# Attention's split and values one and two steps later, and v turned by VectorE through a DRAM scratch instead of TensorE

## The chip, the cores and the metric

The kernel runs on one core of a Trainium2 chip. The time is the device time of one execution in microseconds (us); a version is told by the median over its runs. Beside it stands one profiled execution, with a trace of every instruction and DMA.

## The reference

One layer of a streaming encoder on 320 frames (256 of a prompt and 64 of a running stream), D = 2048, all in float32:

```
xn = RMSNorm(x)
h  = xn @ w_in                     # columns [u 2048 | v 2048 | q 2048 | k 256 | v_attn 256]
u, v = gelu(h[u]), gelu(h[v])
a  = u * (ws_masked @ LayerNorm(v) + bs)       # mixes tokens inside chunks of 128
o  = windowed attention of q on k, v_attn      # 32 heads of 64, 4 groups, rope, sinks
x  = x + (sigmoid(xn @ w_gate_a) * (a @ w_a) + sigmoid(xn @ w_gate_b) * (o @ w_b)) @ w_out
x  = x + (silu(RMSNorm(x) @ w_fg) * (RMSNorm(x) @ w_fu)) @ w_fd
y  = RMSNorm(x)                    # outputs also: new keys, new values, LayerNorm(v) of the 64 frames
```

What matters here is v: LayerNorm runs over its 2048 features, and the mixing runs over tokens, so v is needed with tokens on the partitions, while a product leaves it with features on the partitions.

## The kernel before

**Products.** Activations lie with features on the partitions: `xh` and `xl` (high and low part, [128, 16, 320]). `gemm` (from L136 on) makes 512 output features at a time: four PSUM banks of [128, 320], and for each pair of 128-row blocks of the weight it loads [128, 2, 512] floats (`raw`, 512 KB, `fetch`, issued on SyncE's queue, SP), splits it (`prepare`, `split`: ScalarE copies the high part `hi`, L107; VectorE subtracts to make the low part `lo`, L110) and runs 24 matmuls, three for each product of two parts (L151 to L153). The split runs two blocks ahead, the fetch six; there are four `raw` and three `hi` and `lo` buffers.

**Order.** After every 12 matmuls `pump` is called: one slot. `later(n, fn)` writes fn into a calendar, n slots on; at that slot fn's instructions are put into the program. A product of 16 rows of weight has 16 slots. Engines run their queues in order; the program order comes from this calendar, and a scheduler that models the engines may let an instruction whose inputs it holds ready pass one on the same engine that waits. The products come in the order k and v_attn ("kv"), q0, q1, v0, q2, v1, q3, v2, v3, then the four of w_gate for B (gb), of w_branch_b (bb), u, w_gate for A, w_branch_a, w_out and the feed-forward part.

**Attention.** `q_done(g)` begins when the product of q group g is done; `QK0[g]` slots later come the scores of the first of five query chunks, and a chunk every 5 slots. `attend` gives the steps of a chunk with their slots: scores 0 (eight matmuls, maxima, exp into `pr`), weigh 2, pack 3 (VectorE transposes 32x32 blocks of `pr` into `u`, L498), spread 4 (four DMAs on SP write `u` to a DRAM scratch `pd`, L507), gather 6 (one or two DMAs on SP read it back as `pf` with keys on the partitions, L516), part 9 (splits `pf` into `ph` and `pl`, and a half block into `p`), values 11 (two or three matmuls into the bank `o`, L539; ScalarE copies one half, VectorE adds, L541 and L547).

**v.** `v_done(g)` begins when the product of v group g is done. VectorE multiplies by the norm's factor (L577), ScalarE applies gelu (L578). Slots 3 to 6 turn one of the four tiles each: three TensorE transposes into the bank `vt` (L583), a VectorE copy of 256 columns (L585) and a ScalarE copy of 128 (L586) into `tok`, which holds tokens on the partitions. At slot 8 come the statistics for LayerNorm (`stats`, L592).

**After v3.** `at` is 16: `open_late` opens the next pool, `split_o` splits the attention output in eight steps for bb, `v_aggr` joins the statistics, `v_norm` normalises v.

Of the kernel before, what the change touches and what calls it, by code (L numbers as in the profile page):

```python
# [10 lines left out]
F32 = mybir.dt.float32  # L11
F32R = mybir.dt.float32r
AF = mybir.ActivationFunctionType
# [5 lines left out]
P = 128  # L19
D = 2048  # L20
DC = D // P
T = 320
TS = 64
F = 5632
FC = F // P
W = 512
# [8 lines left out]
    [(0, 4), (512, 4), (1024, 4), (1536, 2), (1792, 2)],  # L35
]
QV = [("q", 0), ("q", 1), ("v", 0), ("q", 2), ("v", 1), ("q", 3), ("v", 2), ("v", 3)]
QK0 = [14, 24, 18, 13]

NK = [64, 128, 192, 192, 192]  # L40
KC = [0, 0, 0, 64, 256]
# [3 lines left out]
def f32(ap):  # L45
    return ap.bitcast(F32)
# [23 lines left out]
def tile_hybrid_step(ctx: ExitStack, tc: tile.TileContext, a: dict, outs: list):  # L70
    nc = tc.nc
    y_p, y_s, ko_p, vo_p, ko_s, vo_s, gv_s = outs
    w_in, w_gate = a["w_in"][0], a["w_gate"][0]
# [7 lines left out]
    dram = ctx.enter_context(tc.tile_pool(name="dram", bufs=1, space=DRAM))  # L81

    def bank(name):
        return psum.tile([P, 512], F32, tag="bank", name=name)
# [5 lines left out]
    def later(slots, fn):  # L90
        calendar.setdefault(now[0] + max(1, slots), []).append(fn)
# [13 lines left out]
    def split(hi, lo, src, eng=None):  # L105
        if eng is None:
            nc.scalar.activation(hi, src, AF.Copy)  # L107
        else:
            eng.tensor_copy(hi, src)
        nc.vector.tensor_tensor(lo, src, f32(hi), op=ALU.subtract)  # L110


    plan = []
    for w, c0, k0, nk, nt in products(a):
        plan += [(w, c0, k0 + kb, nt) for kb in range(0, nk, 2)]
    raws, parts = {}, {}
    at_block = [0]

    def fetch(j):
        if j < len(plan):  # L120
# [4 lines left out]
                w[k * P : (k + 2) * P, c0 : c0 + nt * P].rearrange("(c p) m -> p c m", p=P),  # L125
            )

    def prepare(j, eng=None):
        if j < len(plan):
            n = plan[j][3] * P  # L130
            hi = wpool.tile([P, 2, W], F32R, tag="hi", name=f"hi_{j}", bufs=PARTS)
            lo = wpool.tile([P, 2, W], F32R, tag="lo", name=f"lo_{j}", bufs=PARTS)
            split(hi[:, :, :n], lo[:, :, :n], raws.pop(j)[:, :, :n], eng)
            parts[j] = hi, lo

    def gemm(w, c0, xh, xl, name, k0=0, nk=DC, nt=4):  # L136
        ps = [bank(f"mm_{name}_{t}") for t in range(nt)]
        for kb in range(0, nk, 2):
            j = at_block[0]
            at_block[0] += 1  # L140
            assert plan[j][1:] == (c0, k0 + kb, nt)
            if j + PARTS - 1 not in parts:
                prepare(j + PARTS - 1)
            fetch(j + PARTS - 1 + RAWS)
            hi, lo = parts.pop(j)
            for t in range(nt):
                cols = slice(t * P, (t + 1) * P)
                for c in range(2):
                    k = kb + c
                    o = ps[t][:, :T]  # L150
                    nc.tensor.matmul(o, hi[:, c, cols], xh[:, k, :], start=(k == 0), stop=False)  # L151
                    nc.tensor.matmul(o, hi[:, c, cols], xl[:, k, :], start=False, stop=False)  # L152
                    nc.tensor.matmul(o, lo[:, c, cols], xh[:, k, :], start=False, stop=(k == nk - 1))  # L153
                if nt == 1 or t % 2 == 1:
                    pump()
        return [p[:, :T] for p in ps]


    ident = main.tile([P, P], F32, name="ident")
# [6 lines left out]
    tok = main.tile([P, 3, D], F32, name="tok")  # L166
# [6 lines left out]
    xs = [(i, P if i < 2 else TS) for i in range(3)]  # L173
# [96 lines left out]

    x_in(0)
    prepare(0, nc.vector)
    x_in(1)
    fetch(RAWS)
    x_keep(0)
    x_in(2)
    prepare(1)
    fetch(RAWS + 1)
    for k in range(3, DC):
# [49 lines left out]
    def rope_turn(t0):  # L329
        t1 = tmp.tile([P, 2, T], F32, tag="st", name="rope_t1")  # L330
        cb = cos_t.unsqueeze(1).broadcast_to([P, 2, T])
        sb = sin_t.unsqueeze(1).broadcast_to([P, 2, T])
        q2 = qr[:, t0 : t0 + 2, :]
        nc.vector.tensor_tensor(q2, q2, cb, op=ALU.mult)
        nc.vector.tensor_tensor(t1, swp[:, t0 : t0 + 2, :], sb, op=ALU.mult)
        nc.vector.tensor_tensor(q2, q2, t1, op=ALU.add)
# [118 lines left out]
    def attend(g, n, qs, st):  # L455
# [38 lines left out]
        nb = nk // 32  # L494
# [54 lines left out]
                    pov[0:64, e], olv[:, e], op=ALU.add  # L549
                )  # L550

        return ((0, scores), (2, weigh), (3, pack), (4, spread), (6, gather), (9, part), (11, values))

    def q_done(g, ps):
        for t in range(4):
            nc.scalar.activation(qr[:, t, :], ps[t], AF.Copy)
        qs = ap.tile([P, 20, 2, 64], F32R, tag="qs", name=f"qs_{g}")
        hi, lo = q_parts(g, qs)
        later(1, lambda: rope_swap(4))
        later(5, lambda: rope_turn(0))  # L560
        later(7, lambda: rope_turn(2))
        at = QK0[g]
        later(at - 5, lambda: hi(0))
        later(at - 4, lambda: lo(0))
        later(at - 3, lambda: hi(1))
        later(at - 2, lambda: lo(1))
        for n in range(5):
            for dt, step in attend(g, n, qs, {}):
                later(at + 5 * n + dt, step)
# [4 lines left out]
    def v_done(g, ps):  # L574
        for t in range(4):
            v = tmp.tile([P, T], F32, tag="e1", name=f"v_{g}_{t}", bufs=4)
            nc.vector.tensor_tensor(v, ps[t], rx, op=ALU.mult)  # L577
            nc.scalar.activation(v, v, AF.Gelu_apprx_tanh)  # L578

            def turn(t=t, v=v):  # L580
                pt = bank(f"vt_{g}_{t}")
                for i, n in xs:
                    nc.tensor.transpose(pt[:n, i * P : (i + 1) * P], v[:, i * P : i * P + n], ident)  # L583
                c = slice((4 * g + t) * P, (4 * g + t + 1) * P)
                nc.vector.tensor_copy(tok[:, 0:2, c], pt[:, 0:256].rearrange("p (i c) -> p i c", i=2))  # L585
                nc.scalar.activation(tok[0:64, 2, c], pt[0:64, 256:384], AF.Copy)  # L586

            later(3 + t, turn)

        def stats():  # L590
            for i, n in xs:
                nc.vector.bn_stats(bst[:n, i, g, :], tok[:n, i, g * W : (g + 1) * W])  # L592

        later(8, stats)

    for c, g in QV:
        if c == "q":
            q_done(g, gemm(w_in, 2 * D + g * W, xh, xl, f"q{g}"))
        else:
            v_done(g, gemm(w_in, D + g * W, xh, xl, f"v{g}"))  # L600
# [13 lines left out]
    def split_o(m):  # L614
        for k in range(m, m + 2):
            split(late["yh"][:, k, :], late["yl"][:, k, :], f1[:, k, :])
# [36 lines left out]
            nc.vector.memset(late["wst"][64:128, :, 0:64], 0.0)  # L653

    at = 16
    later(at - 3, open_late)
    for k in range(0, DC, 2):
        later(at - 3 + k // 2 + 1, lambda k=k: split_o(k))
    later(at + 3, v_aggr)
    for g in range(4):  # L660
        later(at + max(1, 9 * g - 2), lambda g=g: v_load(g))
# [20 lines left out]
    for g in range(4):  # L682
        ps = gemm(w_bb, g * W, yh, yl, f"bb{g}")
        for t in range(4):
            m = 4 * g + t
# [48 lines left out]
    for g in range(4):  # L734
        ps = gemm(w_ba, g * W, yh, yl, f"ba{g}")
        for t in range(4):
            m = 4 * g + t
# [21 lines left out]
    for g in range(4):  # L759
        ps = gemm(w_out, g * W, xh, xl, f"wo{g}")  # L760
        for t in range(4):
            m = 4 * g + t
# [46 lines left out]
    for nf in FPARTS:  # L809
        for g in range(nf // 4):  # L810
            c0 = f0 * P + g * W
# [13 lines left out]
        for c0, nt in DOWN[last]:  # L825
            ps = gemm(w_fd, c0, xh, xl, f"fd{f0}_{c0}", k0=f0, nk=nf, nt=nt)
            for t in range(nt):
                m = c0 // P + t
# [26 lines left out]
    for h in range(2):  # L855
        c = slice(h * D // 2, (h + 1) * D // 2)
# [61 lines left out]
```

## Time and profile before

| | us |
|---|---|
| median of 3 runs | 1968.05 (1966.51 to 1968.14) |
| the profiled execution, its own time | 1968.4 |
| its span, first to last instruction | 1966.6 |
| mean granted TensorE clock | 0.995 |
| kv product begins | 8.5 |
| q0 to v3 (eight products) | 46.5 to 319.4 |
| gb (four products) | 319.4 to 441.1 |
| bb (four products) | 441.1 to 553.7 |

A row of the page or of a view names line, engine and operation, then the tile written and the tiles read, then shapes and the count. PE is TensorE's matmuls, PEld its weight loads, DVE VectorE, ACT ScalarE, POOL GpSimd, SP SyncE's queue; a q behind the engine stands for its sequencer. In a row of waits stands who waited for whom: us in total, how often, and the longest. In a timeline stand start and length in us; in square brackets the idle time ahead of it and what ended it. Matmuls are pipelined: the length of one is not its cost; the distance of two starts is.

### The profile page before, as it was taken

To read this page: it belongs to the slowest core of one execution; us is meant where nothing else is said; L and a number is where in the kernel's file an instruction comes from. 1 tells how busy PE (TensorE), PEld (TensorE's weight loads), DVE (VectorE), ACT (ScalarE), POOL (GpSimd) and SP (SyncE) were. 2 spreads that over 40 slices of the span, in tenths; PEclk is the share of its full clock that TensorE was granted. 3 is DMA by queue.
4 is the path that set the end of the run, shared out by engine and by line. 5 is a ranking of instruction groups with operands and counts; after the bars stand their busy time and mean duration, and the time that the engine had idled before them with its cause. 6 is when DMAs were issued, how large, how long until landed. Compare 5 with 4: busy or idle time off the path is not lost.

```text
span 1966.6 us, 31779 instructions
## 1 busy us (share of the span) xinstructions
PE 1937.0 (98%) x13179; PEld 1924.8 (98%) x13179; DVE 1042.1 (53%) x1527; ACT 813.6 (41%) x1220; POOL 4.7 (0%) x12
## 2 busy tenths in 40 slices
PE   9999999999999999999999999999999999999996
PEld 8999989999999999999999999999999999999996
DVE  5778887953444543455465444443444444444454
ACT  5566766633333443333343333333333333333343
POOL 0000000000000000000000000000000000000000
PEclk9999999999999999999999999999999999999998
DMA  8555666754444444445445555445555544555433
GB/s 268 155 160 171 181 169 170 218 159 153 147 142 137 138 150 150 150 150 203 150 150 151 150 150 150 150 150 150 150 149 147 154 149 150 146 151 149 152 130 102
DMA packets 169457, 307.41 MB, mean 156 GB/s; under 512 B 11313, under 2 KB 28673, under 8 KB 169121
## 3 DMA queue, kind: packets, MB, share of 16 engines
q1 hardware_dynamic: 164256, 293.64, 49.2%
q10 hardware_dynamic: 5056, 11.74, 1.9%
q8 instruction: 103, 1.69, 0.4%
q14 instruction: 42, 0.34, 0.1%
HBM read 292.15 MB, written 12.45 MB: 155 GB/s over the span
## 4 chain that ended last, share of the span: by engine, by line
PE 82%; DVE 0%; ACT 0%; issue 0%; DVEq 0%
PE mm_fd L151 5%; PE mm_fu L151 5%; PE mm_fg L151 5%; PE mm_fd L153 5%; PE mm_fu L153 5%; PE mm_fg L153 5%; PE mm_fg L152 5%; PE mm_fu L152 5%; PE mm_fd L152 5%; PE mm_u L151 2%; PE mm_bb L151 2%; PE mm_bb L153 2%; PE mm_ba L152 2%; PE mm_ga L152 2%; PE mm_wo L152 2%; PE mm_wo L153 2%
## 5 line engine op out<-in xcount | busy, mean ns | idle before, releaser
L110 DVE TENSOR_TENSOR lo<-raw,hi 128x1024 fp32r<-128x1024 f32 (+1 forms) x534 | 646.2, 1211 | 661.9 <-ACT hi L107 660.4
L107 ACT ACTIVATE hi<-raw 128x1024 fp32r<-128x1024 f32 (+1 forms) x533 | 559.4, 1050 | 1023.4 <-PE mm_fu L152 188.8
L151 PE MATMUL mm_fd<-xh,hi 128*128 128x320 f32 x704 | 218.2, 310 | 0.0
L151 PE MATMUL mm_fg<-yh,hi 128*128 128x320 f32 x704 | 217.8, 309 | 0.0
L153 PE MATMUL mm_fg<-yh,lo 128*128 128x320 f32 x704 | 217.5, 309 | 0.0
L151 PE MATMUL mm_fu<-yh,hi 128*128 128x320 f32 x704 | 217.5, 309 | 0.0
L152 PE MATMUL mm_fu<-yl,hi 128*128 128x320 f32 x704 | 217.5, 309 | 0.0
L153 PE MATMUL mm_fu<-yh,lo 128*128 128x320 f32 x704 | 217.5, 309 | 0.0
L152 PE MATMUL mm_fg<-yl,hi 128*128 128x320 f32 x704 | 217.5, 309 | 0.0
L153 PE MATMUL mm_fd<-xh,lo 128*128 128x320 f32 x704 | 217.1, 308 | 0.0
L152 PE MATMUL mm_fd<-xl,hi 128*128 128x320 f32 x704 | 217.1, 308 | 0.0
L151 PEld LDWEIGHTS mm_fg<-yh,hi 128*128 128x128 f32 x704 | 132.2, 188 | 0.1
L152 PEld LDWEIGHTS mm_fg<-yl,hi 128*128 128x128 f32 x704 | 132.2, 188 | 0.1
L153 PEld LDWEIGHTS mm_fg<-yh,lo 128*128 128x128 f32 x704 | 132.2, 188 | 0.0
L151 PEld LDWEIGHTS mm_fu<-yh,hi 128*128 128x128 f32 x704 | 132.1, 188 | 0.0
L152 PEld LDWEIGHTS mm_fu<-yl,hi 128*128 128x128 f32 x704 | 132.1, 188 | 0.0
L153 PEld LDWEIGHTS mm_fu<-yh,lo 128*128 128x128 f32 x704 | 132.1, 188 | 0.0
L152 PEld LDWEIGHTS mm_fd<-xl,hi 128*128 128x128 f32 x704 | 132.1, 188 | 0.0
L151 PEld LDWEIGHTS mm_fd<-xh,hi 128*128 128x128 f32 x704 | 132.1, 188 | 0.0
L153 PEld LDWEIGHTS mm_fd<-xh,lo 128*128 128x128 f32 x704 | 132.1, 188 | 0.0
L151 PE MATMUL mm_q<-xh,hi 128*128 128x320 f32 x256 | 81.3, 318 | 0.0
L151 PE MATMUL mm_u<-xh,hi 128*128 128x320 f32 x256 | 80.3, 314 | 0.0
(256 smaller groups left out, 3935.2 us busy)
## 6 DMA issues: line engine op xcount, KB each, us to landing
raw<-in_w_in_dram SPq DMA_DIRECT2D x104, 512.0 KB, 3.8
raw<-in_w_ffn_gate_dram SPq DMA_DIRECT2D x88, 512.0 KB, 3.6
raw<-in_w_ffn_up_dram SPq DMA_DIRECT2D x88, 512.0 KB, 3.6
raw<-in_w_ffn_down_dram SPq DMA_DIRECT2D x82, 512.0 KB, 3.6
raw<-in_w_gate_dram SPq DMA_DIRECT2D x64, 512.0 KB, 3.7
raw<-in_w_branch_b_dram SPq DMA_DIRECT2D x32, 512.0 KB, 3.7
raw<-in_w_branch_a_dram SPq DMA_DIRECT2D x32, 512.0 KB, 3.7
raw<-in_w_out_dram SPq DMA_DIRECT2D x32, 512.0 KB, 3.9
```

The lines of the kernel that those rows point to most:

```text
L107: nc.scalar.activation(hi, src, AF.Copy)
L110: nc.vector.tensor_tensor(lo, src, f32(hi), op=ALU.subtract)
L151: nc.tensor.matmul(o, hi[:, c, cols], xh[:, k, :], start=(k == 0), stop=False)
L152: nc.tensor.matmul(o, hi[:, c, cols], xl[:, k, :], start=False, stop=False)
L153: nc.tensor.matmul(o, lo[:, c, cols], xh[:, k, :], start=False, stop=(k == nk - 1))
```

## The change

Four things.

1. In `attend`, part moves from slot 9 to 10 and values from 11 to 13. Group q3 begins its chunks one slot earlier (`QK0[3]` 12 instead of 13).
2. The turn of v leaves TensorE. `turn` is now three VectorE transposes of 32x32 blocks per tile, two of [128, 128] and one of [128, 64], which write `tok` at every fourth element (16 bytes apart). Then `spread` (slot 7) issues twelve DMAs on SP that write the blocks to a DRAM scratch `vd`, in runs of 128 floats, and `gather` (slot 9) two DMAs on SP that read it back into `tok`, and GpSimd clears rows 64 to 127 of the last token block. `stats` moves from slot 8 to 13.
3. The columns of the v weights are interleaved as they are split: tile t of a v product holds every fourth column, 4m + t. `hi` and `lo` of the 32 v blocks are written in order, but `raw` is read in steps of four floats (16 bytes) by ScalarE and VectorE.
4. `open_late` and the eight `split_o` come one slot later.

```diff
-QK0 = [14, 24, 18, 13]
+QK0 = [14, 24, 18, 12]
...
+    def is_v(j):
+        w, c0, _, _ = plan[j]
+        return w.shape == w_in.shape and D <= c0 < 2 * D
...
-            split(hi[:, :, :n], lo[:, :, :n], raws.pop(j)[:, :, :n], eng)
+            h, l, r = hi[:, :, :n], lo[:, :, :n], raws.pop(j)[:, :, :n]
+            if is_v(j):
+                h, l = (x.rearrange("p c (t m) -> p c t m", t=4) for x in (h, l))
+                r = r.rearrange("p c (m t) -> p c t m", t=4)
+            split(h, l, r, eng)
...
-        return ((0, scores), (2, weigh), (3, pack), (4, spread), (6, gather), (9, part), (11, values))
+        return ((0, scores), (2, weigh), (3, pack), (4, spread), (6, gather), (10, part), (13, values))
...
             def turn(t=t, v=v):
-                pt = bank(f"vt_{g}_{t}")
-                for i, n in xs:
-                    nc.tensor.transpose(pt[:n, i * P : (i + 1) * P], v[:, i * P : i * P + n], ident)
-                c = slice((4 * g + t) * P, (4 * g + t + 1) * P)
-                nc.vector.tensor_copy(tok[:, 0:2, c], pt[:, 0:256].rearrange("p (i c) -> p i c", i=2))
-                nc.scalar.activation(tok[0:64, 2, c], pt[0:64, 256:384], AF.Copy)
+                vb = v.rearrange("p (b r) -> p b r", r=32)
+                for i in range(2):
+                    nc.vector.transpose(blocks[:, i, :, :, t], vb[:, 4 * i : 4 * i + 4, :])
+                nc.vector.transpose(blocks[:, 2, 0:2, :, t], vb[:, 8:10, :])
...
+        c = slice(g * W, (g + 1) * W)
+        blocks = tok[:, :, c].rearrange("p i (b c t) -> p i b c t", b=4, t=4)
+        vd = dram.tile([T, W], F32, tag="vd", name=f"vd_{g}", bufs=2)
+
+        def spread():
+            for a_ in range(4):
+                r, x = slice(32 * a_, 32 * a_ + 32), slice(128 * a_, 128 * a_ + 128)
+                for i, nb in ((0, 4), (1, 4), (2, 2)):
+                    nc.sync.dma_start(
+                        vd[P * i : P * i + 32 * nb, x].rearrange("(b r) x -> r b x", r=32),
+                        tok[r, i, c].rearrange("p (b x) -> p b x", b=4)[:, 0:nb, :],
+                    )
+
+        def gather():
+            nc.gpsimd.memset(tok[TS:P, 2, c], 0.0)
+            nc.sync.dma_start(tok[:, 0:2, c], vd[0:256, :].rearrange("(i p) x -> p i x", p=P))
+            nc.sync.dma_start(tok[0:TS, 2, c], vd[256:T, :])
...
-        later(8, stats)
+        later(7, spread)
+        later(9, gather)
+        later(13, stats)
...
-    later(at - 3, open_late)
+    later(at - 2, open_late)
     for k in range(0, DC, 2):
-        later(at - 3 + k // 2 + 1, lambda k=k: split_o(k))
+        later(at - 2 + k // 2 + 1, lambda k=k: split_o(k))
```

## The prediction

> **What bounds the kernel now.** I read the page first, then busy time by stretches, the waits of TensorE, its timeline around the longest waits, and last the rows of the operations that are exchanged.
>
> ```profile
> span 1966.6 us, 31779 instructions
> ## 1 busy us (share of the span) xinstructions
> PE 1937.0 (98%) x13179; PEld 1924.8 (98%) x13179; DVE 1042.1 (53%) x1527; ACT 813.6 (41%) x1220; POOL 4.7 (0%) x12
> ```
>
> TensorE bounds the whole, so an edit counts only by what it adds to or takes from TensorE's row. The next rows, busy time in three stretches, show where that row holds more than dense products: the eight q and v products, the four gb products, and the four bb products beside which nothing else runs on TensorE.
>
> ```profile
> 46.50:319.40 272.90, 265.07 (x1785) 258.57 (x1784) 214.86 (x411) 176.01 (x409) 0.00 (x0) 0.99 0.59 169
> 319.40:441.10 121.70, 119.17 (x808) 117.23 (x807) 89.54 (x146) 62.34 (x96) 0.00 (x0) 1.00 0.62 185
> 441.10:553.70 112.60, 112.60 (x769) 112.60 (x769) 45.92 (x49) 35.04 (x35) 0.00 (x0) 1.00 0.46 150
> ```
>
> The columns are: stretch, its length, busy time of PE, PEld, DVE, ACT and POOL, granted clock, DMA share, GB/s. Four dense products take 112.6 us, so one takes 28.15 and one of its 192 matmuls 0.147. Eight take 225.2, but the first stretch lasts 272.9: 47.7 us go to attention, turns, waits and a clock of 0.99. The second has 9.1 us of the same. All that the change can win is in these 57 us. TensorE is idle in 272.90 - 265.07 = 7.8 and 121.70 - 119.17 = 2.5 us of them. The waits of TensorE between 106 and 352 us name this idle time:
>
> ```profile
> PE o L539 <- ACT ph L107: 4.9, 3, 2.4
> PE o L539 <- DVE p L110: 3.2, 6, 1.2
> PE vt L583 <- ACT pr L478: 1.3, 1, 1.3
> PE o L539 <- DVE pl L110: 0.8, 3, 0.3
> ```
>
> The sum is 10.2 of 10.3 us. The values matmuls (o) wait 8.9 us for the split probabilities ph, pl and p; a turn of v waits once for a PSUM bank that the exp of attention (pr) still reads. TensorE's timeline shows what may follow a long wait:
>
> ```profile
> 146.89 0.49 PE L539 MATMUL o<-ph,vv 128*128 128x512 f32 x1 [1.47 <-ACT ph L107]
> ...
> 149.83 0.47 PE L151 MATMUL mm_q<-xh,hi 128*128 128x320 f32 x1
> 150.10 0.47 PE L152 MATMUL mm_q<-xl,hi 128*128 128x320 f32 x1
> ...
> 287.93 0.50 PE L539 MATMUL o<-ph,vv 128*128 128x512 f32 x1 [2.41 <-ACT ph L107]
> ```
>
> After the first wait, dense matmuls start 0.27 us apart instead of 0.147. The next rows, the same columns by stage (v0, q2, v1, q3, v2, v3, and the first product gb0), show a clock of 0.96 in q2 and 0.95 in v3, the stages of these two waits.
>
> ```profile
> 106.60:139.10 32.50, 31.90 (x222) 31.37 (x221) 23.33 (x48) 18.30 (x54) 0.00 (x0) 1.00 0.59 169
> 139.10:178.60 39.50, 37.19 (x240) 35.50 (x239) 33.15 (x64) 28.85 (x67) 0.00 (x0) 0.96 0.56 164
> 178.60:212.50 33.90, 32.70 (x224) 31.82 (x224) 29.19 (x53) 22.25 (x52) 0.00 (x0) 1.00 0.67 191
> 212.50:247.40 34.90, 34.62 (x237) 33.43 (x236) 27.73 (x59) 24.20 (x62) 0.00 (x0) 1.00 0.59 166
> 247.40:283.50 36.10, 35.08 (x238) 34.03 (x237) 31.82 (x57) 22.79 (x54) 0.00 (x0) 1.00 0.66 178
> 283.50:319.60 36.10, 33.69 (x225) 33.06 (x224) 25.43 (x54) 23.98 (x60) 0.00 (x0) 0.95 0.55 160
> 319.60:352.00 32.40, 29.87 (x197) 27.95 (x196) 24.91 (x46) 22.09 (x44) 0.00 (x0) 1.00 0.62 177
> ```
>
> A clock of 0.96 over 39.5 us loses 1.6 us, and of 0.95 over 36.1 about 1.8; I take 1.5 each. The VectorE column is the second thing to see: 195.6 of 245.4 us, and 33.15 of 39.5 in q2. TensorE is the bound, but VectorE is close behind it here.
>
> **Turns off TensorE.** One turn now stands in TensorE's timeline like this:
>
> ```profile
> 154.25 0.31 PE L153 MATMUL mm_q<-xh,lo 128*128 128x320 f32 x1
> 154.40 0.49 PE L583 MATMUL vt<-ident,v 128*128 128x128 f32 x3
> 154.65 0.40 PE L151 MATMUL mm_q<-xh,hi 128*128 128x320 f32 x1
> 154.88 0.31 PE L152 MATMUL mm_q<-xl,hi 128*128 128x320 f32 x1
> ```
>
> From 154.40 to 154.88 there are 0.48 us, of which one dense matmul would take 0.147. A turn costs 0.33, sixteen cost 5.3 us, and these go whatever else happens, for nothing on TensorE replaces them. The bank wait of 1.3 us goes too: no turn asks for a PSUM bank any more. **The turns' new price** lies on VectorE and SyncE. The rows are the copies that go (from the rows of vt), transposes of two sizes, and the weight split of a block (from the rows of raw):
>
> ```profile
> L585 DVE COPY tok<-vt x16: 383/418/426, 151.9 to 339.0; 128x256 f32<-128x256 f32 x16
> L586 ACT ACTIVATE tok<-vt x16: 250/270/273, 154.1 to 339.5; 64x128 f32<-64x128 f32 x16
> L498 DVE STREAM_TRANSPOSE u<-pr 128x768 f32<-128x768 f32 x12 | 11.7, 973 | 0.6 <-ACT pr L492 0.3
> L498 DVE STREAM_TRANSPOSE u<-pr 128x256 f32<-128x256 f32 x4 | 1.8, 442 | 1.7 <-ACT pr L492 1.7
> L107 ACT ACTIVATE hi<-raw x55: 1042/1059/1098, 108.6 to 347.9; 128x1024 fp32r<-128x1024 f32 x55
> L110 DVE TENSOR_TENSOR lo<-raw,hi x55: 1160/1219/1227, 109.7 to 349.4; 128x1024 fp32r<-128x1024 f32 x55
> ```
>
> A transpose costs (973 - 442) / 512 = 1.04 ns an element over a base of 176. A turn has two of 128 elements (309 ns) and one of 64 (243): 0.86 us, 13.8 for sixteen, against 16 x 0.418 = 6.7 for the copies. VectorE gains 7.1 us of work; ScalarE loses 16 x 0.27 = 4.3. Their writes step 16 bytes, which no row shows; if each element cost twice, 320 x 1.04 ns x 16 = 5.3 us more.
>
> **Interleaved columns.** The 32 blocks of v are split from raw read in steps of 16 bytes. No row of this trace reads SBUF at such a step. The bounds for lo are 1.22 us, the contiguous row, and 1.22 + 1024 x 1.04 ns = 2.28, a second element time for each element. I take the first, since no row shows an element of f32 costing two; I keep the second as a rival, for it decides the sign. [...]
>
> **Queues.** SyncE (SP) gets twelve spreads and two gathers for each v, on the queue that fetches the weights and carries attention's own scratch.
>
> ```profile
> ACT ph L107 <- DMA pf<-pd: 6.9, 7, 2.3
> SPq L123 <- DVE lo L110: 84.6, 37, 5.8
> L507 SPq DMA_DIRECT2D pd<-u x80: 312/441/1307, 108.9 to 338.8; - x80
> pd<-u SPq DMA_DIRECT2D x48, 96.0 KB, 3.5
> raw<-in_w_in_dram SPq DMA_DIRECT2D x42, 512.0 KB, 4.5
> pf<-pd SPq DMA_DIRECT2D x16, 256.0 KB, 4.2
> ```
>
> Twelve issues at 0.44 take 5.3 us, then the gather waits some 3.5 us for the last landing, and behind it in SP stand the weight fetches and the next pd and pf. A fetch has four blocks of 24 x 0.147 = 3.5 us before its split, 14.1, less 4.5 for landing and 0.4 for issue: 9.2 us of room (the 84.6 us row shows SP waiting for buffers, not the reverse). One fetch stands between spread and gather, the next behind the gather; each is late by some 4 us, 6 to 7 where a pd and a pf stand among them. I cost this at nothing. It is tight for attention of q3 beside the turn of v2: spreads and pf at slot 135, gather at 137, pd at 138. At 2 us a slot, pd goes out about 5 us late, and pf lands near 21 us after slot 135 where its part is due at 18. ScalarE then waits 3 us at ph, with later weight splits queued behind it; values has three slots, 6 us, against 3 + 2.6 for the four splits. It just fits: 1 us for it. GpSimd's clearing of the unused rows waits for the spreads; its queue is empty there and no soon work reads them, so nothing. The later statistics, the later late pool and the output splits (one slot) end well before bb reads them: nothing.
>
> **Part one slot, values two slots later.** ScalarE waits 6.9 us in seven places for pf, at most 2.3. A slot is 12 dense matmuls, 1.76, with the extras about 2. One more slot before part covers all but the end of these waits; one more between part and values covers the 1.2 us of p and 0.3 of pl. Of 8.9 us I take 7. With those waits I let both low-clock stretches go, 3.0 us; only the two longest waits were followed by one (the 1.2 and 1.3 us ones were not). If the first comes from something else, 1.5 stays.
>
> **The sum.** -5.3 (turns) - 1.3 (bank) - 7 (values) - 3 (clock) = -16.6. VectorE then has 195.6 + 7.1 = 202.7 us in 228.8, 89%, and q2 needs 33.15 + 1.8 of it in a stage of about 34.4: I put back 3 us there and 1 for the late pf. That makes -12.6. The profiled execution took 1968.4 us, 1.8 more than its span and 0.35 over the median of 1968.05; 1968.4 - 12.6 = 1955.8, so 1956. Own range: 1950 (nothing put back, all 8.9 us gone) to 1962.
>
> **Rivals.** (1) *The strided read costs a second element time, and VectorE becomes the bound.* 32 x 1.06 = 34 us more: 202.7 + 34 = 237 us in a stretch that TensorE could do in 229. Stage by stage the need is about 37 in q2 and v1 and 40 in v2, against 39.5, 33.9 and 36.1 now. At 95% busy, 237 / 0.95 = 249 instead of 245.4; with idle left as chains need it, up to 256: 1972 to 1979, most likely 1974. It decides from where VectorE passes 95% of 229 = 217 us, that is 15 us over 32 blocks, or a lo of 1.7 us. Lo-buffers two blocks ahead soften it, and stages with room (q3, v0) take some: part of its chance lies at no change or a small gain. For it: nothing measured here speaks against it. [...] (2) *The waits only move.* Values stay late because ScalarE and VectorE, in order and fuller, are late by two slots as well, or pf is late behind the spreads. Then only the turns and the bank pay: -6.6, 1962, between 1959 and 1966. For it: releasers ph and p are these two engines. Against: no wait was over 2.4 us, and up to 4 are given. (3) *The change does not take effect in the queue*: values move in program order, but TensorE's queue may keep them where they were. That gives the same 1962 and I count it with (2).
>
> **Numbers.** Forecast 0.46, rival 1 0.37, rival 2 with 3 0.17. Some 0.2%, 3.9 us, is what a measurement of this kernel tells from no change. Faster by more: 0.45 + 0.08 + 0.12 = 0.65. Within: 0.01 + 0.12 + 0.04 = 0.17. Slower: 0.17 + 0.01 = 0.18. The range reaches from 1950 over rival 2 to 1975, which takes in the larger half of rival 1; the likeliest case alone has 1950 to 1962.
>
> **What would show it.** In the changed profile: no vt rows with v; the q and v stretch near 259 us, its waits of o under 2 us and the clock 1.00; transposes of 0.31 and 0.24 us; hi and lo of v blocks at 1.06 and 1.22. A lo of v over 1.7 us, with VectorE above 95% in v1 and v2 and dense matmuls waiting for lo, proves rival 1; waits of o that stay near 9 us prove rival 2; dense matmuls or hi that wait for raw would prove the cost of the queue wrong.

## The result, and the profile after

The changed kernel takes 1984.52 us in the median of four runs (1983.04 to 1988.78), against 1968.10 before (1966.51 to 1968.59, four runs): 16.4 us slower, a ratio of 1.0088 with a 95% interval of 1.0071 to 1.0106. The forecast was 1956, with a range from 1950 to 1975.

The page after, with the columns of the page before:

```profile
span 1981.3 us, 31766 instructions
...
PE 1938.4 (98%) x13131; PEld 1923.5 (97%) x13131; DVE 1070.5 (54%) x1559; ACT 842.7 (43%) x1204; POOL 6.8 (0%) x16
```

VectorE has 28 us more to do and ScalarE 29 more. For ScalarE the change only took work away, 4.3 us of copies, so that number alone says that something it does became dearer. The rows of raw, between 106 and 370 us of the changed kernel, name it:

```profile
L110 DVE TENSOR_TENSOR lo<-raw,hi x57: 1181/1991/2065, 104.4 to 369.1; 128x1024 fp32r<-128x1024 f32 x57
L107 ACT ACTIVATE hi<-raw x56: 1042/2030/2104, 109.5 to 367.4; 128x1024 fp32r<-128x1024 f32 x56
```

The line numbers of the split are unchanged, so the rows can be held against those of before. The shortest are still 1.04 and 1.18 us: the blocks of q and gb. More than half of the blocks in this region belong to v, so the median is one of theirs: 2.03 us for hi (1.06 before) and 1.99 for lo (1.22). A step of 16 bytes costs ScalarE 0.95 ns more for each of 1024 elements and VectorE 0.75.

Where TensorE's time went shows in busy time by stage: first the q and v products and gb as a whole, then q2, v1, v2 and v3:

```profile
46.50:335.10 288.60, 268.54 (x1758) 259.04 (x1757) 239.78 (x429) 204.46 (x396) 1.57 (x3) 0.97 0.61 171
335.10:456.00 120.90, 116.97 (x788) 115.24 (x787) 93.06 (x160) 63.05 (x94) 0.52 (x1) 1.00 0.67 202
139.20:179.50 40.30, 36.00 (x226) 33.87 (x226) 33.58 (x70) 31.71 (x73) 0.52 (x1) 0.97 0.73 203
179.50:215.50 36.00, 33.61 (x224) 32.29 (x224) 33.21 (x49) 26.18 (x41) 0.00 (x0) 0.99 0.61 170
251.70:293.40 41.70, 34.08 (x211) 32.09 (x209) 34.40 (x50) 31.91 (x48) 0.00 (x0) 0.91 0.58 159
293.40:335.10 41.70, 39.16 (x247) 37.74 (x247) 34.78 (x71) 30.39 (x66) 0.53 (x1) 0.93 0.59 171
```

The first stretch grew from 272.9 to 288.6 us; gb did not grow. Two things are to be seen. TensorE is idle for 20.1 us of the first row instead of 7.8. And the clock column lost more: 0.03 x 40.3 + 0.01 x 36.0 + 0.09 x 41.7 + 0.07 x 41.7 = 8.2 us in these four stages, against 3.4 before. The waits of TensorE between 46 and 460 us name the idle time:

```profile
PE o L548 <- ACT ph L107: 6.2, 3, 2.5
PE o L548 <- DVE pl L110: 4.8, 6, 1.4
PE s L473 <- DVE qs L460: 3.2, 1, 3.2
PE mm_gb L160 <- DVE v L586: 2.5, 1, 2.5
PE mm_v L162 <- DVE lo L110: 2.1, 4, 0.9
PE o L548 <- DVE p L110: 1.8, 6, 0.5
PE s L473 <- DVE v L586: 1.3, 1, 1.3
PE mm_q L160 <- ACT pr L487: 1.2, 2, 0.6
PE mm_q L162 <- DVE lo L110: 0.7, 1, 0.7
```

The sum is 23.8 us, 13.6 more than the 10.2 of before. The waits of values (o) did not shrink with two more slots but grew from 8.9 to 12.8. New rows stand beside them: scores wait for the split q (qs) and for VectorE's read of v's bank (v), q and gb products for pr and v, which are no operands of theirs but read PSUM banks, and dense matmuls for lo. All releasers are ScalarE and VectorE. So 13.6 us of waits and 4.8 of clock were lost and 5.3 of turns won: 13.1 of the 14.7 us by which the span grew.

VectorE was not full, though: 33.2 of 36.0 us in v1, 34.4 of 41.7 in v2. Its longest idle time in that region tells why. The first row is of before (106 to 352 us), the second of after (106 to 370):

```profile
DVE lo L110 <- ACT hi L107: 9.2, 12, 1.9
```

```profile
DVE lo L110 <- ACT hi L107: 20.6, 18, 3.0
```

Each lo needs its hi, and hi itself now takes 2.03 us. VectorE stands waiting at the head of its queue: before the lo at 258.99 us it was idle for 2.62 us, and the transpose of a pr that had been ready since 256.7 us began only behind that lo, at 260.90. So what stands behind lo in the queue (pl, p, qs, nm, f) is late though the engine had time for it.

### The profile page after: what moved, and what is told of

It reads as the page before. It is cut to its first block, busy times and chain, and to the rows that moved or that the text cites. A ratio compares the mean times of both kernels' runs of the same rounds, so it can differ in the third digit from the quotient of the medians.

```text
span 1981.3 us, 31766 instructions
## 1 busy us (share of the span) xinstructions
PE 1938.4 (98%) x13131; PEld 1923.5 (97%) x13131; DVE 1070.5 (54%) x1559; ACT 842.7 (43%) x1204; POOL 6.8 (0%) x16
## 4 chain that ended last, share of the span: by engine, by line
PE 83%; DVE 3%; ACT 1%; issue 1%; DVEq 0%; ACTq 0%
PE mm_fd L160 5%; PE mm_fu L161 5%; PE mm_fg L161 5%; PE mm_fd L161 5%; PE mm_fg L160 5%; PE mm_fu L160 5%; PE mm_fg L162 5%; PE mm_fu L162 5%; PE mm_fd L162 5%; PE mm_u L160 2%; PE mm_ba L162 2%; PE mm_bb L162 2%; PE mm_ba L160 2%; PE mm_bb L161 2%; PE mm_wo L162 2%; PE mm_ga L162 2%
## 5 line engine op out<-in xcount | busy, mean ns | idle before, releaser
L110 DVE TENSOR_TENSOR lo<-raw,hi 128x1024 fp32r<-128x1024 f32 (+1 forms) x534 | 671.9, 1259 | 671.9 <-ACT hi L107 670.0
L107 ACT ACTIVATE hi<-raw 128x1024 fp32r<-128x1024 f32 (+1 forms) x533 | 591.4, 1110 | 1010.5 <-PE mm_fu L161 188.8
L162 PE MATMUL mm_v<-xh,lo 128*128 128x320 f32 x256 | 80.2, 316 | 2.1 <-DVE lo L110 2.1
```

## The experiments

Three theories stood at first. S: the reads at 16-byte steps cost. Q: the scratch transfers on SP cost. M: the moved slots cost. Ratios are to the kernel before, run beside it on the same chip; a difference in us between two experiments can be one between two chips, on which the kernel before had medians from 1967.7 to 1969.2.

**The slots alone** (part 10, values 13, `QK0[3]` 12, output splits one later, on the kernel before):

> The kernel before with the slot moves alone: part at 10, values at 13, q3 one slot earlier, the output splits one slot later; the turn of v stays on TensorE and the columns stay in order. Theory S (the reads at 16-byte steps double hi and lo of the v blocks and fill ScalarE and VectorE): the moves are harmless and win back most of the 8.9 us that values waits for, so 1957 to 1964 us. Theory Q (the scratch transfers on SyncE's queue make pf and the weights late): the same. Theory M (the moves themselves bring PSUM banks into each other's way: scores, gb and q products waited for banks in the changed kernel): 1968 or more.

Measured 1968.90 us, ratio 1.0005 (0.9995 to 1.0014): no change. The win of S and Q doesn't come; M's bound is met, though without a loss. The longest waits of TensorE and one line of its timeline:

```profile
PE o L539 <- ACT pr L478: 4.5, 1, 4.5
PE vt L583 <- ACT pr L478: 3.3, 1, 3.3
PE o L539 <- DVE p L110: 1.2, 1, 1.2
```

```profile
154.89 0.80 PE L539 MATMUL o<-ph,vv 128*128 128x512 f32 x1 [4.49 <-ACT pr L478]
```

The slots do what was forecast of them: values waits 1.4 us for its splits instead of 8.9. But values and a turn now wait 7.8 us in two places for the exp of the scores (pr). It is no operand of either. All PSUM tiles of this kernel come from one pool of eight banks (`bank`), and a step that takes a bank waits until what lay in it has been read, so a bank that pr still reads fits both waits. A new wait took the old one's place.

**Reads in order**, all else as changed:

```diff
-            if is_v(j):
-                h, l = (x.rearrange("p c (t m) -> p c t m", t=4) for x in (h, l))
-                r = r.rearrange("p c (m t) -> p c t m", t=4)
```

> The changed kernel with raw of the v blocks read in order, so v's features land in the wrong places; transposes, scratch, slots stay. Theory S: hi and lo return to 1.06 and 1.22 us and the time falls by 20 to 30 us from 1984.5, to 1955 to 1964. Theory Q: the time stays within 5 us of 1984.5. Theory M: it stays above 1968.

Measured 1957.25 us (1956.63 to 1958.20), ratio 0.9949 (0.9934 to 0.9964), with hi at 1.06 and lo at 1.22 us. S holds: taking out the step alone turns a loss of 16.4 us into a gain of 10. The scratch, the transposes and the slots are all still there, so Q and M fall as causes of the loss; what M said of the banks stays, as a price on the slots beside the old turn.

**No scratch transfers**, the steps kept (`later(7, spread)` and `later(9, gather)` left out):

> The changed kernel without the twelve spreads, the two gathers and the clearing of each v, so the blocks of v stay where VectorE's transposes put them; the reads at 16-byte steps stay. Theory S: 1978 to 1985 us, hi and lo at 2.0 us. Theory Q: 1955 to 1964. Theory M: 1975 or more.

Measured 1984.54 us, ratio 1.0088 (1.0073 to 1.0103), the same as with them. Q falls; S and M both allow this time. The fourteen DMAs of each v on SP's queue cost nothing that can be seen beside the steps.

**The steps alone**, on the kernel before (only `is_v` and the rearranged split added):

> The kernel before with the reads at 16-byte steps alone; the turn on TensorE and the slots stay, so v's features land in the wrong places. Theory S: hi and lo of the v blocks at 2.0 us, the time 15 to 30 us above 1968. Theories Q and M: 1968 to 1972, the longer splits hidden.

Measured 1997.61 us, ratio 1.0152 (1.0135 to 1.0169): 30 us, at the upper end of S, with hi at 2.05 and lo at 2.00 us. The steps cost more here than in the changed kernel, where they cost 27.

**The steps on one engine each**, on the changed kernel. For ScalarE alone:

```diff
+                nc.scalar.activation(h4, r4, AF.Copy)
+                nc.vector.tensor_tensor(l, r, f32(h), op=ALU.subtract)
```

> The changed kernel with the 16-byte steps in ScalarE's hi alone; VectorE's lo reads in order, so the values of v's products are wrong. ScalarE has room (204 of 289 us busy), but lo waits for hi: if the loss comes from the chain hi to lo, more than half of it stays, 1970 to 1980 us. If VectorE's fullness is the loss, 1957 to 1965.

and for VectorE alone:

```diff
+                nc.scalar.activation(h, r, AF.Copy)
+                nc.vector.tensor_tensor(l4, r4, f32(h4), op=ALU.subtract)
```

> The changed kernel with the 16-byte steps in VectorE's lo alone; ScalarE's hi reads in order, so the values of v's products are wrong. If VectorE's fullness is the loss (240 of 289 us busy): 1970 to 1980 us. If the chain behind hi on ScalarE is: 1960 to 1966.

(In the second, hi and lo still add up to the interleaved weight, other than the expectation says.) Measured 1971.67 us, ratio 1.0017 (1.0008 to 1.0027), and 1973.22, ratio 1.0030 (1.0019 to 1.0040). The rows of the two splits, first with ScalarE's step, then with VectorE's:

```profile
L142 ACT ACTIVATE hi<-raw x31: 2003/2058/2110, 105.7 to 316.2; 128x1024 fp32r<-128x1024 f32 x31
L143 DVE TENSOR_TENSOR lo<-raw,hi x31: 1194/1225/1228, 107.8 to 318.3; 128x1024 fp32r<-128x1024 f32 x31
```

```profile
L143 DVE TENSOR_TENSOR lo<-raw,hi x31: 1973/2016/2046, 104.3 to 317.9; 128x1024 fp32r<-128x1024 f32 x31
L142 ACT ACTIVATE hi<-raw x30: 1041/1058/1088, 109.5 to 315.4; 128x1024 fp32r<-128x1024 f32 x30
```

VectorE's waits for hi between 106 and 352 us, with ScalarE's step:

```profile
DVE lo L143 <- ACT hi L142: 19.2, 20, 2.6
DVE lo L110 <- ACT hi L107: 4.2, 3, 3.0
```

Against 1957.25 with neither, the step costs 14.4 us on ScalarE and 16.0 on VectorE; both together cost 27.3. Each engine's share is about half, and each time came out where its own theory had put it. "VectorE is full" can't be the whole mechanism, for in the first of these VectorE has no more to do than in the fast one. There it waits 23.4 us for hi, against 8.4 in the same region with the reads in order, which fits the chain from hi to lo. With VectorE's step it waits only 7.5, so that half of the loss is the length of lo itself. What a longer hi does to ScalarE's other steps, which stand behind it in the queue, is not told apart from the chain.

**A full version without a 16-byte step.** The blocks of v are turned in runs of 32 floats, the scratch leaves `tok` in a permuted order of features, and `v_norm` puts it right as it writes:

```diff
-        blocks = tok[:, :, c].rearrange("p i (b c t) -> p i b c t", b=4, t=4)
+        blocks = tok[:, :, c].rearrange("p i (b t c) -> p i b t c", b=4, t=4)
...
-        nc.vector.tensor_tensor(v, v, gb[:n, 0, :], op=ALU.mult)
-        nc.vector.tensor_tensor(v, v, gb[:n, 1, :], op=ALU.add)
+        y = y.rearrange("p (a t c) -> p a t c", a=4, t=4)
+        v = v.rearrange("p (t a c) -> p a t c", a=4, t=4)
+        gb = gb.rearrange("p k (t a c) -> p k a t c", a=4, t=4)
+        nc.vector.tensor_tensor(y, y, gb[:n, 0], op=ALU.mult)
+        nc.vector.tensor_tensor(v, y, gb[:n, 1], op=ALU.add)
```

> A full version without any 16-byte step: weights split in order, VectorE's transposes write runs of 32 floats, the scratch goes as in the change and leaves tok in a permuted order of features, and v_norm puts the order right as it writes (runs of 32 floats, one more buffer, no more instructions). Theory S (the reads at 16-byte steps are the whole loss): 1955 to 1960 us, as with the contiguous reads alone (1957), and clearly faster than before. If the time of the contiguous run came from leaving the permutation out, this is 1962 or more.

Measured 1956.27 us (1954.40 to 1958.75), ratio 0.9944 (0.9932 to 0.9957): 11 us faster than before, the best of all full versions. Its waits of TensorE:

```profile
PE o L545 <- DVE pl L110: 1.3, 2, 0.8
PE s L470 <- DVE qs L457: 1.1, 1, 1.1
PE o L545 <- DVE p L110: 0.9, 3, 0.5
PE mm_q L159 <- DVE lo L110: 0.7, 1, 0.7
PE s L470 <- DVE v L583: 0.3, 1, 0.3
```

That is 4.3 us in all, and none for a bank that pr reads.

**The same version at the slots of before:**

> The same version with the slots of before (part 9, values 11, q3 and the output splits as they were). If the later slots win what values waited for once the turns have left TensorE's PSUM banks: 1961 to 1966 us, some 5 to 8 us slower than with the later slots, with waits of o near 9 us. If the later slots win nothing here either, as beside the old turn: within 2 us of it.

Measured 1966.73 us, ratio 0.9995 (0.9986 to 1.0004): no change from before, with 11.8 us of waits of o:

```profile
PE o L545 <- ACT ph L107: 5.2, 4, 1.9
PE o L545 <- DVE pl L110: 3.4, 6, 1.1
PE o L545 <- DVE p L110: 3.2, 6, 1.2
```

So the new turn alone wins nothing, the later slots alone win nothing, and both together win 11 us.

**No turn at all**, at the later slots and at those of before (`later(3 + t, turn)` left out), to price the turn itself:

> The kernel before with the slot moves and without any turn of v: no transposes, no copies, no scratch, so tok keeps the input in place of v. If the later slots only pay once the turns leave TensorE's PSUM banks free (bank theory): 1950 to 1957 us, with less than 4 us of waits of o. If the later slots are worth nothing by themselves and the gain of the full version came from elsewhere: 1961 to 1964.

> The kernel before without any turn of v, at the slots of before, so tok keeps the input in place of v. By the prediction's terms the turns and their bank wait are worth 5.3 + 1.3 us, so 1961 to 1963 us, with some 9 us of waits of o left. If the turns' matmuls were hidden in these waits, it is 1965 or more.

Measured 1959.71 us, ratio 0.9958 (0.9943 to 0.9973), and 1968.59, ratio 1.0002 (0.9993 to 1.0012). The first lies between its two cases; the slots are worth some 9 us without a turn, and the waits of o are 1.0 us. The second time seems to say that with the slots of before even leaving the turn out wins nothing. But the edit does one thing more. Without a turn nothing writes `tok` before the statistics of LayerNorm (bst) read it, so they have moved to the start of the program, where VectorE waits in them for the input x and the first product begins late. The first two rows are of the run at the slots of before, the third is of the kernel before:

```profile
8.89 0.69 DVE L591 BATCH_NORM_STATS2 bst<-tok 128x6 f32<-128x512 f32 x1 [2.29 <-DMA tok<-in_x_prompt_dram]
12.05 0.60 PE L151 MATMUL mm_kv<-xh,hi 128*128 128x320 f32 x1 [5.17 <-DVE hi L109]
```

```profile
8.49 0.60 PE L151 MATMUL mm_kv<-xh,hi 128*128 128x320 f32 x1 [0.61 <-DVE hi L109]
```

In their profiles q0 begins at 49.0 us here and at 50.2 in the run with the later slots, instead of 46.5. The order of instructions belongs to the program, so I take it that every execution of these two kernels pays some 3 us of this, and that 1959.71 would be near 1956 without it, in the first case (an estimate from the profiles). From q0 to the start of bb the second kernel takes 393.2 us instead of 394.6, so 1.4 of the prediction's 6.6 us come. The waits of TensorE show where the rest went:

```profile
PE o L539 <- ACT ph L107: 6.4, 3, 2.6
PE o L539 <- DVE pl L110: 2.7, 5, 0.8
PE o L539 <- DVE p L110: 1.8, 7, 0.6
PE mm_gb L153 <- DVE lo L110: 0.9, 1, 0.9
PE mm_gb L151 <- ACT hi L107: 0.4, 1, 0.4
```

They are 12.2 us in all instead of 10.2, though the bank wait of 1.3 is gone: TensorE reaches the same late operands earlier and waits for them longer. The clock stands at 0.50 for 10.2 us of this stretch instead of 6.8, which loses another 1.7. So 5.3 - 2.0 - 1.7 = 1.6, close to the 1.4 of this one profile.

**The step on TensorE instead**, raw, hi and lo in order:

```diff
-                cols = slice(t * P, (t + 1) * P)
+                cols = slice(t, W, 4) if is_v(j) else slice(t * P, (t + 1) * P)
```

> The changed kernel with raw, hi and lo of the v blocks in order and the 16-byte step moved to TensorE, whose weight load for tile t reads every fourth column of hi and lo; nothing is left out. Theory S (steps cost the vector engines, 30 us): if a weight load at this step still fits beside the matmul ahead of it (188 of its ns overlap already), 1955 to 1960 us. If it costs TensorE too, each of the 768 matmuls of v grows by up to 0.05 to 0.1 us: 1995 to 2035 us.

Measured 2011.94 us, ratio 1.0223 (1.0208 to 1.0239): it costs TensorE too. A row of weight loads and two neighbours of the timeline:

```profile
L157 PEld LDWEIGHTS mm_v<-xh,hi x256: 308/330/332, 108.7 to 368.5; 128*128 128x128 f32 x128
```

```profile
114.86 0.40 PE L159 MATMUL mm_v<-xh,lo 128*128 128x320 f32 x1
115.10 0.40 PE L157 MATMUL mm_v<-xh,hi 128*128 128x320 f32 x1
```

The load of a strided tile takes 0.33 us instead of 0.19, and two matmuls start 0.23 to 0.24 us apart instead of 0.147. Of the 0.14 us by which the load grew, 0.09 show in the distance of the matmuls.

**A bank for each turn**, added to the full version: one TensorE transpose and a copy of eight columns per turn.

> The version with VectorE's turn and no 16-byte step, and beside it, at each of the sixteen turns, one PSUM bank taken as the old turn took it: one TensorE transpose instead of three and a copy of 8 columns by VectorE, whose result nobody uses. The transposes themselves are worth 16 x 0.15 to 0.2, some 3 us: 1958 to 1960 if nothing else matters. Bank theory (a turn's bank puts TensorE behind the exp of the scores, as 4.5 and 3.3 us in the kernel with the slots alone): 1962 to 1969, with waits of vt or o on pr.

Measured 1961.35 us, ratio 0.9962 (0.9949 to 0.9976), where the version without them had 0.9944 (0.9932 to 0.9957). By its own time that is between the two cases. But the kernel before had a median of 1969.16 beside it, and against that the win is 7.8 us instead of 11.5: 3.7 us less, close to the 3 of the first case, and the two intervals overlap. So the time does not speak for the bank theory. Some of the waits do:

```profile
PE o L545 <- DVE es L478: 2.7, 1, 2.7
PE o L545 <- ACT ph L107: 1.6, 2, 1.0
PE o L545 <- DVE p L110: 1.4, 3, 0.9
PE vt L589 <- DVE vtop L590: 1.3, 1, 1.3
```

Two of these four releasers, es and vtop, are no operands of what waits, 4.0 us in all; vtop is the copy that reads a turn's bank, and values start at 152.21 us, right behind es at 152.02 and vtop at 151.91. That these steps wait for a bank which a turn has taken fits this. But of the waits on pr, which the theory named, only 0.2 us came. Shown is that the old turn takes away what the later slots win (1968.90 with it, 1959.71 without), and that waits for no operand come and go with the turns' banks; that these waits are the whole of it is not shown.

## Why the prediction was wrong

**The failed step** is "I take the first, since no row shows an element of f32 costing two", of the interleaved columns: it put the price of the strided read at nothing. The step cost ScalarE 0.95 ns and VectorE 0.75 ns more for each element: lo took 1.99 us where 1.22 was taken and 2.28 was the upper end, and hi took 2.03, for which the prediction expected 1.06 and weighed no other bound. Together this is 27.3 us of time, the difference between 1984.52 and the 1957.25 of the reads in order. That no row shows a cost was no evidence, for no row showed the step either.

**Rival 1** named this cause, but its price of 1974 was 10 us short. It counted only lo. Hi on ScalarE was left out of the sum, and it is half the loss (14.4 us alone against 16.0 for lo). Its mechanism was half right too: VectorE did not pass 95% (92% in v1, 82% in v2). Half of the loss is lo's own length on VectorE, as it said; the other half comes with hi, for which VectorE stands waiting with the attention steps queued behind. The sum also held no loss of clock: beside the longer waits 4.8 us more of it went (8.2 against 3.4), where 3 were to be won. The sign of rival 2, waits of o near 9 us, came as well (12.8), but as an effect of the steps: with the reads in order they are 3.7.

**Right together, wrong one by one** was the rest. With the reads in order the time is 1957.25, and 1956.27 in the full version, against a forecast of 1956. In the profile of the full version the waits of o fell by 6.7 us where 7 were taken, and the bank wait of 1.3 is gone. The clock won 1.7 where 3 were taken (one stretch of 3.4 us at 0.50 is left, after the wait of 1.1 us for qs), and new waits cost 2.1 where 4 were put back: two misses that cancel, so the last microsecond is luck. But the terms do not hold singly, as the sum had them. That "these go whatever else happens" of the turns failed: the turns alone won nothing (1966.73 us), since values still waited, for longer. "Of 8.9 us I take 7" failed as a term by itself: with the old turns in place the slots alone won nothing (1968.90), for 7.8 us of waits on pr stood where the waits for operands had been. Each edit takes away what hides the other's gain. A bank wait of values was in no rival.

**The queue** was costed right, at nothing: without the scratch transfers the time is the same (1984.54). In the full version, without the steps, the transfers are there too and the forecast's time comes. The transposes were 0.39 and 0.28 us where 0.31 and 0.24 stood, for their writes step 16 bytes; in the full version, which writes runs of 32, they are 0.27 and 0.20. Over all of them that is 5.2 us more, the size that the prediction had named for elements that cost twice (5.3) and then left out of its sum. It did not matter for the time: 1957.25 with it and 1956.27 without.

## What to carry to other kernels

When an edit changes an access pattern, look for the innermost step in bytes, of reads on every engine that touches the data, before counting instructions; where no row shows such a step, measure one instruction with it first: here that price decided more than the rest of the sum. Gains of edits that relieve waits on one path do not add: price each with the other's limit still in place, and try them together before dropping either. An interleave that an engine would do element by element could be moved here to where it costs runs of 32, into the norm that rewrites the data anyway. And an experiment that leaves a step out may let other steps move: look at the start of its timeline before pricing the step by it.

## What the runs showed of the hardware

- A read of f32 at a step of 16 bytes takes ScalarE 2.03 us and VectorE 1.99 us for 1024 elements, against 1.06 and 1.22 in order (2.06 and 2.02 where the row holds blocks of v alone). VectorE's 32x32 transposes of 128 elements take 0.39 us with writes at that step and 0.27 with runs of 32.
- TensorE's weight load of a 128x128 tile at that step takes 0.33 us instead of 0.19, and matmuls of 320 columns start 0.23 us apart instead of 0.147.
- In these traces the clock fell for short stretches around waits of TensorE in the middle of dense work. Before the change it stood at 0.50 from 149.0 to 152.4 us and from 288.9 to 292.3, after waits of 1.47 and 2.41 us; waits of 1.20 and 1.02 us were not followed by one. In the changed kernel three waits within 3 us (1.31, 0.22 and 0.45) were followed by such a stretch too, and in the full version one of 1.1; a wait of 2.45 us ahead of gb, at 338.9 us of the changed kernel, was not, so the length of a single wait does not decide it. The stages q2, v1, v2 and v3 of the changed kernel lost 8.2 us to it, q2 and v3 of the kernel before 3.4.
